# Computing the state-space branch output by block products, with token sums beside the other branches

## The chip, the cores and the metric

The kernel runs on one core of one Trainium2 chip. Its time is that of one execution on the device, in microseconds, as the median over repeated runs. Besides the timed runs there is one execution taken by the hardware profiler. All rows of the profile below come from that single execution, and it has a time of its own, given beside the span of its instructions in the table further down.

## The reference, cut to what matters

One layer of a streaming encoder runs over 1024 tokens of width 1024 in float32. A projection feeds three branches (latent attention, forgetting attention and a state-space scan) and a gate for each. The branch outputs are merged with sigmoid gates, projected and added to the input. A gated feed-forward block follows.

```python
y_a = mla_branch(u_mla, ...) @ w_br_mla[l]          # 512 inner columns
y_b = fox_branch(u_fox, ...) @ w_br_fox[l]          # 512 inner columns
y_c = ssm_branch(u_ssm, ...) @ w_br_ssm[l]          # 1024 inner columns
merged = g[:, :, 0] * y_a + g[:, :, 1] * y_b + g[:, :, 2] * y_c
x = x + merged @ w_out[l]
x = x + conv_ffn(rms_norm(x, norm_ffn_g[l]), ...)
```

`ssm_branch` ends in `rms_norm(y * silu(z), norm_g)`, so its last step is a multiplication of each of the 1024 inner columns by its own element of `norm_g`. The change concerns this scale and the three products with `w_br_fox`, `w_br_mla` and `w_br_ssm`, above all the last.

## The kernel before, in words

Every matrix product keeps float32 accuracy by splitting both operands into a rounded high half and the remainder, its low half. A product over one block of 128 inner rows is then three matmuls, high by high, high by low and low by high (`mm3`, L161 to L168, whose matmuls all have L167). A split is `split` (L139): ScalarE copies the source into the high half (L142) and VectorE subtracts that from the source to give the low half (L143). Inner dimensions are cut in blocks of 128 partitions, tokens in halves of 512 columns.

The stages follow each other on TensorE: input projections, attention, the scan, the branch products, the output projection (`wo`, L1443) and the feed-forward. The gate projections are a generator, `all_fill` (L866), whose matmuls are laid between those of attention and scan. Its last ones run behind the scan's last. Each gate block ends in a tanh on ScalarE (L873) that takes its bias from the constant tile `pc_g`, and in a store to `g_d`.

The scan handles 8 chunks of 128 tokens. `ssd_c` (L1237 to L1245) ends each: eight 128x128 transposes into two PSUM tiles (L1242), one ScalarE copy of each PSUM tile into the tile `yT` (L1243), and a store of `yT` to the DRAM tile `ys_d` (L1245). `yT` has one buffer; `ssd_b` of the next chunk uses it for a square (L1229), which therefore waits for the store.

The branch stage (L1269 to L1312) follows. For branch 1 (fox), 0 (mla) and 2 (state-space) it first loads the branch's output in blocks of 128 rows by 1024 tokens (`ar`, L1283) and splits each into `ah` and `al`; for branch 2 the split multiplies by the column of `pc_n` (L1287, L1288). Then it goes through 8 output tiles of 128 columns. Each takes a load and split of a weight tile (`load_w`, L758, into `wr`, `wh`, `wl`, two buffers each), a load of the gate (`gl`, L1298), and per token half a product into one of six PSUM banks (`ybr`), with 12 matmuls for branches 1 and 0 and 24 for branch 2. VectorE multiplies by the gate (L1305). GpSimd adds for branch 0 (L1308) and VectorE for branch 2 (L1310). For branch 2 the sum is split into `hnh` and `hnl` (L1311, L1312), which the output projection reads. In all these are 2x8x2x12 + 8x2x24 = 768 matmuls of 128x512.

The tiles `ar`, `gl` and the gate projections' results share one tag, `t4`, with four buffers of 4 KB per partition. A load into `t4` can be issued only when one of the four is free.

Two kinds of order exist. In a section under `manual_schedule` the named engines run in the order in which the program was written. Everything else, here all of SP's transfers, all of GpSimd, and in the branch stage also TensorE, VectorE and ScalarE, is put in order by the planner before the launch, from its own estimate of when each operation is ready. Each engine then runs its list strictly in that order. The scan holds TensorE alone to the program order. The output projection does the same. In the feed-forward, a product by seven block products per pair of output tiles is in use already (`product`, L1392; sums of weight tiles by GpSimd at L1492 to L1496; `ua`, `ub`, `uc`, `ud` at L1397).

Pools are stacked: when one closes, the next to open lies at the same address. At L1269 `mix` closes, which held `const2` (L62). The pool opened after it begins where `const2` began. In `const2`, allocated in order from L94, `lead2`, `identb`, `ones`, `tri`, `strict`, `mssd`, `mfox` and `mmla` take 3360 bytes per partition, and `pc_g` the next 336. Before the change that place is taken by the first two `merged` tiles, which are written by the first L1305.

## Time and profile before

| | |
|---|---|
| median of 3 runs | 2069.3 us (2063.23 to 2069.39) |
| the profiled execution | 2072.75 us, span of its instructions 2071.0 us |
| TensorE busy | 2016.5 us, 97% of the span, 10250 matmuls |
| VectorE, ScalarE, GpSimd busy | 1432.4 us, 949.4 us, 616.3 us |
| first and last matmul of the branch stage start | 1152.4 us and 1326.6 us |
| mean granted TensorE clock | 0.992 of full speed |

Times in rows are microseconds unless marked ns. `PE` is TensorE, `PEld` its weight load, `DVE` VectorE, `ACT` ScalarE, `POOL` GpSimd, `SP` the engine that issues all transfers and `SPq` its queue. A row of the chain of waits gives a start, a length and what ran. A row of the timeline gives start, length, engine, line, operation, output and inputs, and in brackets the idle time before it and what ended that. A row of the groups by shape gives the count, the total and the mean in ns, and after the next bar the idle time before. A row of the stages gives the stretch, its length, the busy time of PE, PEld, DVE, ACT and POOL with counts, the granted clock, the share of DMA time and GB/s. Matmuls overlap: each is shown with 389 ns, though the next starts earlier. PE busy near the length of a stretch so means that no matmul waited, and the time per matmul is read from a row that holds many.

### The profile page before, as it was taken

The numbers are of one execution on the slowest core, as the hardware profiler recorded it, in microseconds if no ns is written. First come the engines' busy times: TensorE is split into PE (matmuls) and PEld (weight loads), VectorE is DVE, ScalarE is ACT, GpSimd is POOL, SyncE is SP. The second block draws the span as 40 slices with busy tenths as digits, with TensorE's granted clock in tenths as the row PEclk, the third lists the DMA queues.
The fourth block names the chain that finished last, engine by engine and source line by source line (L and its number), as shares of the span: only waits on it lengthen the run. The fifth ranks groups of instructions, "written<-read, shape, count | busy, mean of one in ns | idle before, by whom it ended". The sixth has DMA issues, their size and how long they took to land.

```text
span 2071.0 us, 28992 instructions
## 1 busy us (share of the span) xinstructions
PE 2016.5 (97%) x10250; PEld 1686.1 (81%) x10265; DVE 1432.4 (69%) x2586; ACT 949.4 (46%) x1730; POOL 616.3 (30%) x606
## 2 busy tenths in 40 slices
PE   7999899999999999999999999999899999999999
PEld 7899778788888888787778888888788888878887
DVE  7678479366667767657896355557987777775665
ACT  5555323156556666555554222323454444444432
POOL 4345233222222222210000040002654454422765
PEclk9999999999999999999999999999999999999999
DMA  5158777654434445324442665432222322329675
GB/s 167 45 172 261 260 221 233 204 146 141 118 114 115 130 131 133 100 82 135 134 134 82 215 209 166 153 124 64 77 93 80 96 78 72 102 93 345 218 232 190
DMA packets 274794, 303.62 MB, mean 147 GB/s; under 512 B 18860, under 2 KB 206520, under 8 KB 274648
## 3 DMA queue, kind: packets, MB, share of 16 engines
q1 hardware_dynamic: 274648, 301.76, 47.0%
q8 instruction: 81, 1.33, 0.3%
q14 instruction: 65, 0.53, 0.1%
HBM read 209.03 MB, written 92.67 MB: 146 GB/s over the span
## 4 chain that ended last, share of the span: by engine, by line
PE 81%; DVE 9%; DMA 4%; ACT 2%; issue 2%; POOL 1%; SPq 1%; DVEq 0%; ACTq 0%; POOLq 0%
PE mm L866 17%; PE dn L1729 10%; PE ybr L167 8%; PE ua L1397 5%; PE uc L1397 5%; PE ud L1397 5%; PE fx L167 5%; PE wo L1443 4%; PE s L956 4%; PE tp L1025 3%; PE ub L1397 2%; PE fxv L167 2%; PE q L167 1%; PE kv L167 1%; DMA att_d<-o 1%
## 5 line engine op out<-in xcount | busy, mean ns | idle before, releaser
L866 PE MATMUL mm<-hnh,wh 128*128 128x512 f32 x576 | 250.7, 435 | 0.0
L866 PE MATMUL mm<-hnh,wl 128*128 128x512 f32 x576 | 226.8, 394 | 0.0
L866 PE MATMUL mm<-hnl,wh 128*128 128x512 f32 x576 | 225.4, 391 | 0.0
L978 POOL TENSOR_SCALAR pm<-pm,rs 128x128 f32<-128x128 f32 (+7 forms) x128 | 107.9, 845 | 350.8 <-DVE rs L977 323.7
L1729 PE MATMUL dn<-dr,dr 128*128 128x512 f32 x592 | 182.1, 389 | 0.0
L1031 DVE TENSOR_TENSOR ptl<-tp,pth 128x512 fp32r<-128x512 f32 (+1 forms) x160 | 101.4, 634 | 84.7 <-ACT pth L1030 83.8
L961 DVE TENSOR_REDUCE nmx<-s 128x1 f32<-128x128 f32 (+2 forms) x192 | 105.8, 551 | 58.3 <-PE s L959 46.7
L971 ACT ACTIVATE pm<-s,nmx 128x128 f32<-128x128 f32 (+2 forms) x192 | 109.6, 575 | 56.9 <-DVE nmx L968 38.1
L1729 PEld LDWEIGHTS dn<-dr,dr 128*128 128x128 f32 x592 | 111.2, 188 | 23.0
L866 PEld LDWEIGHTS mm<-hnh,wl 128*128 128x128 f32 x576 | 108.2, 188 | 24.9
L866 PEld LDWEIGHTS mm<-hnl,wh 128*128 128x128 f32 x576 | 109.2, 190 | 18.4 <-issue 4.1
L866 PEld LDWEIGHTS mm<-hnh,wh 128*128 128x128 f32 x576 | 108.9, 189 | 17.8 <-issue 4.1
L1030 ACT ACTIVATE pth<-tp 128x512 fp32r<-128x512 f32 (+1 forms) x160 | 88.2, 551 | 70.4 <-PE tp L1025 69.6
L956 PE MATMUL s<-qk,qk 96*128 96x384 f32 (+5 forms) x480 | 118.1, 350 | 1.9 <-DMA qk<-q_l 0.9
L1308 POOL TENSOR_TENSOR mg<-mg,gl 128x512 f32<-128x512 f32 x16 | 24.9, 1558 | 306.8 <-DVE gl L1305 306.7
L1729 PE MATMUL dn<-dr 128*128 128x512 f32 x296 | 115.3, 389 | 0.0
L143 DVE TENSOR_TENSOR dr<-dr,dr 128x1024 fp32r<-128x1024 f32 x52 | 75.1, 1446 | 50.5 <-ACT dr L142 39.1
L167 PE MATMUL fx<-w5h,hnh 128*128 128x512 f32 x256 | 102.2, 399 | 2.5 <-ACT w5h L142 2.5
L167 PE MATMUL fx<-w5l,hnh 128*128 128x512 f32 x256 | 100.6, 393 | 2.0 <-DVE w5l L143 2.0
L167 PE MATMUL fx<-w5h,hnl 128*128 128x512 f32 x256 | 100.5, 393 | 0.0
L167 PE MATMUL ybr<-al,wh 128*128 128x512 f32 x256 | 99.2, 390 | 0.1
L167 PE MATMUL ybr<-ah,wl 128*128 128x512 f32 x256 | 98.3, 389 | 0.0
(502 smaller groups left out, 5820.9 us busy)
## 6 DMA issues: line engine op xcount, KB each, us to landing
dr<-act_d SPq DMA_DIRECT2D x99, 256.0 KB
wr<-in_ffn_w_up_dram SPq DMA_DIRECT2D x47, 512.0 KB
wr<-in_w_in_dram SPq DMA_DIRECT2D x36, 512.0 KB
g_d<-t SPq DMA_DIRECT2D x24, 512.0 KB
gl<-g_d SPq DMA_DIRECT2D x24, 512.0 KB
ws<-in_ffn_w_down_dram SPq DMA_DIRECT2D x22, 512.0 KB
wsum_d<-ws SPq DMA_DIRECT2D x22, 512.0 KB
act_d<-fa SPq DMA_DIRECT2D x22, 512.0 KB
```

The lines of the kernel that those rows point to most:

```text
L143: return i, le.tensor_sub(l, src, f32(h))
L167: T.matmul(ps, a(k), b(k), start=(i == 0), stop=(i == n - 1))
L866: T.matmul(ps, a[:, k, :], b[half][:, k, :], start=(k == 0 and i == 0), stop=(k == NK - 1 and i == 2))
L956: T.matmul(ps[:, :w], q_[:, qs], k_[:, a:a + w], start=i_ == 0, stop=not last and i_ == len(o.passes) - 1)
L961: later(c + 0.1, lambda ps=ps, ci=ci, a=a, b=b: V.reduce_max(nmx[:, ci:ci + 1], ps[:, :b - a], axis=AX, negate=True))
L971: pss[ci][1][0] = later(c + 0.9 + 0.1 * ci, lambda ci=ci, a=a, b=b: A.activation(p_[:, a:b], pss[ci][0][:, :b - a], AF.Exp, bias=nb, accum ...
L978: G.tensor_scalar(p_[:, 0:n * P], p_[:, 0:n * P], rs[:, 3:4], 0.0, op0=ALU.mult, op1=ALU.add)
L1030: later(c + 0.05, lambda th=th, pt=pt, off=off: A.activation(th[:, :off], pt[:, :off], AF.Copy))
L1031: pl[0] = later(c + 0.6, lambda th=th, tl=tl, pt=pt, off=off: V.tensor_sub(tl[:, :off], pt[:, :off], f32(th[:, :off])))
L1397: T.matmul(ps, a, b, start=first and n == 0, stop=n == 11, skip_group_check=not first)
L1443: T.matmul(p, a, b, start=k == 0 and i == 0, stop=k == NK - 1 and i == 2)
L1729: T.matmul(ps[m], a[:, ts_], b[:, 512:], start=first_ and j == 0 and q == 0, stop=j == NFH - 1 and q == 2, skip_group_check=not first_)
```

## The change

The product of the state-space branch is regrouped. Output tiles j and j+4 (for j from 0 to 3) form a pair. The two weight tiles, each cut into two halves of the inner dimension, and the tokens, cut into two halves of inner rows and of 512 tokens, form a 2x2 by 2x2 block product, done by seven `product` calls of 12 matmuls in place of eight blocks: `a0` (two), `b0` (one), `c0_` (two) and `d0` (two). Sums of weight blocks (`weight_sums`, four GpSimd operations of 128x512 per pair) and sums of token blocks (`tsum[1]` to `tsum[4]`) are the operands; the temporaries `e1`, `f`, `e5`, `X` and `Y` put the results together. The last pair's accumulated tiles are rounded into `mh` and `ml` for the output projection by `rounded`; the tiles of the pairs before it are rounded there too.

The token sums are formed while branches 1 and 0 run. In each of the 16 steps s, `sums_load(s)` loads 4 blocks of 128x128 from `ys_d` by two transfers and subtracts on GpSimd; in step s+1 `sums_take` makes two splits of 128x256 and two subtractions of 128x128 on VectorE. They go into the `hn` tiles that the gate projections read before. Branch 0's blocks are loaded in steps 2 to 5 (`whole`), half of the plain state-space blocks in steps 9 to 12 (`tok_block`), the first pair's weights in step 15.

TensorE, VectorE and ScalarE now keep program order in the whole stage (from the fourth pair's second product on TensorE alone). Branch 1's four blocks are loaded ahead of that section. The operands lie in new pools `slot0` to `slot3` of four 4 KB tiles each, opened before the `mg` pools: `slot0` and `slot1` hold branch 1's high and low halves, then the blocks of token half 0; `slot2` and `slot3` branch 0's.

The scale by `pc_n` moves into the scan's end: the copy of each PSUM tile into `yT` becomes four copies of 128x128, each with its column as scale.

```diff
                 pt = psp.tile([P, 512], F32, name=uid("stp"), tag="ts", bufs=2)
                 for j in range(4):
                     T.transpose(pt[:, j * P:j * P + P], yf[:, (4 * g + j) * P:(4 * g + j + 1) * P], ident)
-                A.activation(o.yT[:, 4 * g:4 * g + 4, :], pt.rearrange("p (j s) -> p j s", j=4), AF.Copy)
+                for j in range(4 * g, 4 * g + 4):
+                    A.activation(o.yT[:, j, :], pt[:, j % 4 * P:j % 4 * P + P], AF.Copy, scale=pc_n[:, j:j + 1])
                 yield 0.44
             SY.dma_start(ys_d[:, :, c * P:c * P + P].rearrange("j p s -> p j s"), o.yT)

...
     mix.close()
+    def product(ps, hl, k0, rh, rl, first=True):
+        n = 0
+        for k in range(4):
+            h, l = hl[0][:, k0 + k, :], hl[1][:, k0 + k, :]
+            for a, b in ((h, rh[k]), (h, rl[k]), (l, rh[k])):
+                T.matmul(ps, a, b, start=first and n == 0, stop=n == 11, skip_group_check=not first)
+                n += 1
+
...
+
+    def weight_sums(S12, S34, ri, rj):
+        G.tensor_add(S12[:, 0:4, :], rj[:, 0:4, :], rj[:, 4:8, :])
+        G.tensor_sub(S12[:, 4:8, :], S12[:, 0:4, :], ri[:, 0:4, :])
+        G.tensor_sub(S34[:, 0:4, :], ri[:, 0:4, :], rj[:, 0:4, :])
+        G.tensor_sub(S34[:, 4:8, :], ri[:, 4:8, :], S12[:, 4:8, :])
+
     with ExitStack() as pe_:
+        slots = [pe_.enter_context(TP(f"slot{i}", 1)) for i in range(4)]
         mgs = [pe_.enter_context(TP(f"mg{i}", 1)) for i in range(4)]
-        mp_ = pe_.enter_context(TP("mgp", 1))
+        trp = pe_.enter_context(TP("tr", 1))
         psp = pe_.enter_context(TP("pse", 6, space=PSUM))
         merged = [mgs[j // 2].tile([P, S], F32, name=f"mg{j}", tag=f"mg{j}") for j in range(NK)]
+
+        def slot(i, shape, d=F32R):
+            return slots[i].tile(shape, d, name=uid("op"), tag="op", bufs=4)
...
         mh, ml = alloc_hn()
-        for b, wsrc, nk in ((1, w_br_fox, 4), (0, w_br_mla, 4), (2, w_br_ssm, 8)):
-            ah, al = [], []
-            for k in range(nk):
-                raw = fpl.tile([P, S], F32, name=uid("ar"), tag="t4", bufs=4)
-                SY.dma_start(raw, ys_d[k] if b == 2 else att_d[b][k * P:k * P + P, :])
-                h = mp_.tile([P, S], F32R, name=uid("ah"), tag="ah", bufs=8)
-                l = mp_.tile([P, S], F32R, name=uid("al"), tag="al", bufs=8)
-                if b == 2:
-                    A.activation(h, raw, AF.Copy, scale=pc_n[:, k:k + 1])
-                    V.scalar_tensor_tensor(out=l, in0=raw, scalar=pc_n[:, k:k + 1], in1=f32(h),
-                                           op0=ALU.mult, op1=ALU.subtract)
-                else:
-                    split(h, l, raw)
-                ah.append(h)
-                al.append(l)
-            wv = wsrc[0].rearrange("(k p) c -> p k c", p=P)
...
-                    V.scalar_tensor_tensor(out=m if b == 1 else g[:, hs], in0=g[:, hs], scalar=1.0, in1=ps,
-                                           op0=ALU.add, op1=ALU.mult)
-                    if b == 0:
-                        G.tensor_add(m, m, g[:, hs])
...
+
+        def sums_load(n):
+            k, q = n // 4, n % 4 * P
+            r = pieces[n] = trp.tile([P, 4, P], F32, name=uid("tr"), tag="tr", bufs=3)
+            for i in range(2):
+                SY.dma_start(r[:, 2 * i:2 * i + 2, :],
+                             ys_d[k + 4 * i].rearrange("p (h c) -> p h c", h=2)[:, :, q:q + P])
+            G.tensor_sub(r[:, 0:2, :], r[:, 1:4:2, :], r[:, 0:2, :])
+
+        def sums_dst(n, a):
+            k, q = n // 4, n % 4 * P
+            return mh[1 - a][:, k:k + 5:4, q:q + P], ml[1 - a][:, k:k + 5:4, q:q + P]
+
+        def sums_take(n, a):
+            r = pieces[n]
+            if a:
+                V.tensor_sub(r[:, 3, :], r[:, 3, :], r[:, 0, :])
+                V.tensor_sub(r[:, 2, :], r[:, 2, :], r[:, 3, :])
+            split(*sums_dst(n, a), r[:, 2 * a:2 * a + 2, :])
+
+        def tok_block(k, half, sl, raw=None):
+            if raw is None:
+                raw = fpl.tile([P, 2, 512], F32, name=uid("ar"), tag="t4", bufs=4)
+            SY.dma_start(raw, ys_d[k:k + 2, :, 512 * half:512 * half + 512].rearrange("k p c -> p k c"))
+            h, l = slot(sl, [P, 2, 512]), slot(sl, [P, 2, 512])
+            split(h, l, raw)
+            return [(h[:, i, :], l[:, i, :]) for i in range(2)]
+
+        def whole(b, k):
+            raw = fpl.tile([P, S], F32, name=uid("ar"), tag="t4", bufs=4)
+            SY.dma_start(raw, att_d[b][k * P:k * P + P, :])
+            h, l = slot(2 * (1 - b), [P, S]), slot(2 * (1 - b) + 1, [P, S])
+            split(h, l, raw)
+            return h, l
+
...
+        def rounded(js, half):
+            for j in js:
+                m = merged[j][:, 512 * half:512 * half + 512]
+                A.activation(mh[half][:, j, :], m, AF.Copy, scale=0.5)
+                V.scalar_tensor_tensor(out=ml[half][:, j, :], in0=m, scalar=0.5, in1=f32(mh[half][:, j, :]),
+                                       op0=ALU.mult, op1=ALU.subtract)
+
+        def operand(raw):
+            h, l = (fpl.tile([P, NK, P], F32R, name=uid(n), tag=n) for n in ("wh", "wl"))
+            split(h, l, raw)
+            return h, l
+
+        def add(o, src, c, half):
+            hs = slice(512 * half, 512 * half + 512)
+            V.scalar_tensor_tensor(out=o.g[c][:, hs], in0=o.g[c][:, hs], scalar=1.0, in1=src,
+                                   op0=ALU.add, op1=ALU.mult)
+            V.tensor_add(merged[c][:, hs], merged[c][:, hs], o.g[c][:, hs])
+
+        def pair_raws(j):
+            o = Head()
+            o.j, o.r = j, [fpl.tile([P, NK, P], F32, name=uid("wr"), tag="wr") for _ in range(2)]
+            for r, c in zip(o.r, (j, j + 4)):
+                SY.dma_start(r, wvs_ssm[:, :, c * P:c * P + P])
+            return o
+
+        def pair_sums(o):
+            o.S12, o.S34 = (fpl.tile([P, NK, P], F32, name=uid(n), tag="t4", bufs=4) for n in ("S12", "S34"))
+            weight_sums(o.S12, o.S34, *o.r)
+
+        def first_operands(o):
+            if o.j:
+                o.hA = operand(o.r[0])
+            o.h22 = last22[:, 0:4, :], last22[:, 4:8, :]
+            split(*o.h22, o.r[1][:, 4:8, :])
+
+        heads = {1: [whole(1, k) for k in range(4)], 0: []}
+        ready = {0: weights(0)}
+        blocks = []
+        order1 = tc.manual_schedule(engines=MANUAL)
+        order1.__enter__()
+        for s in range(2 * NK):
+            b, j = 1 - s // NK, s % NK
+            if s + 1 < 2 * NK:
+                ready[s + 1] = weights(s + 1)
+            g = fpl.tile([P, S], F32, name=uid("gl"), tag="t4", bufs=4)
+            SY.dma_start(g, g_d[b][j])
+            sums_load(s)
+            if s:
+                sums_take(s - 1, 0)
+            wh, wl = ready.pop(s)
+            for half in range(2):
+                hs = slice(512 * half, 512 * half + 512)
+                ps = psp.tile([P, 512], F32, name=uid("ybr"), tag="half")
+                mm3(ps, lambda k: wh[:, k, :], lambda k: wl[:, k, :],
+                    lambda k: heads[b][k][0][:, hs], lambda k: heads[b][k][1][:, hs], 4)
+                m = merged[j][:, hs]
+                V.scalar_tensor_tensor(out=m if b == 1 else g[:, hs], in0=g[:, hs], scalar=1.0, in1=ps,
+                                       op0=ALU.add, op1=ALU.mult)
+                if b == 0:
+                    G.tensor_add(m, m, g[:, hs])
+                if half == 0 and s:
+                    sums_take(s - 1, 1)
+                if half == 0 and 2 <= s < 6:
+                    heads[0].append(whole(0, s - 2))
+                if half == 0 and 9 <= s < 13:
+                    blocks += tok_block(2 * (s - 9), 0, (s - 9) // 2)
+                if half == 0 and s == 2 * NK - 1:
+                    o = pair_raws(0)
+                    o.hA = operand(o.r[0])
+                    pair_sums(o)
...
+        temps = [slot(3, [P, 2, 512], F32) for _ in range(3)]
+        (e1, f), (e5, X), (Y, _) = ([t[:, i, :] for i in range(2)] for t in temps)
+        last22 = slot(3, [P, NK, P])
+        first_operands(o)
+        for a in range(2):
+            sums_take(2 * NK - 1, a)
+        Y11, Y21 = ([[blk[i] for blk in blocks[4 * n:4 * n + 4]] for i in range(2)] for n in range(2))
+        for j in range(4):
+            tail = j == 3
+            a0, d0, c0_, b0 = (halfbank() for _ in range(4))
+            product(a0, o.hA, 0, *Y11)
+            A.activation(e1, a0, AF.Copy)
+            if tail:
+                order1.__exit__(None, None, None)
+                order1 = tc.manual_schedule(engines={mybir.EngineType.PE})
+                order1.__enter__()
+            o.g = {}
+            for c in (j, j + 4):
+                o.g[c] = fpl.tile([P, S], F32, name=uid("gl"), tag="t4", bufs=4)
+                SY.dma_start(o.g[c], g_d[2][c])
+            o.hS12 = operand(o.S12)
+            product(d0, o.h22, 0, *tsum[4])
+            A.activation(f, d0, AF.Copy)
+            if j == 0:
+                last = [tok_block(k, 1, 2, t) for k, t in zip((4, 6), temps[1:])]
+                Y22 = [[blk[i] for blk in last[0] + last[1]] for i in range(2)]
+            product(a0, o.hA, 4, *Y21, first=False)
+            o.hS34 = operand(o.S34)
+            add(o, a0, j, 0)
+            if tail:
+                rounded(range(4), 0)
+            else:
+                nxt = pair_raws(j + 1)
+                pair_sums(nxt)
+            product(c0_, o.hS12, 0, *tsum[1])
+            A.activation(e5, c0_, AF.Copy)
+            G.tensor_sub(Y, e5, f)
+            product(b0, o.hS12, 4, *tsum[2])
+            V.tensor_add(X, b0, e1)
+            if tail:
+                rounded((4, 5, 6), 0)
+            else:
+                first_operands(nxt)
+            product(c0_, o.hS34, 4, *Y22, first=False)
+            V.tensor_add(e1, c0_, X)
+            add(o, e1, j, 1)
+            if tail:
+                rounded(range(4), 1)
+            product(d0, o.hS34, 0, *tsum[3], first=False)
+            V.tensor_add(e5, d0, X)
+            G.tensor_add(Y, Y, e5)
+            add(o, e5, j + 4, 0)
+            if tail:
+                rounded((7,), 0)
+            add(o, Y, j + 4, 1)
+            if not tail:
+                o = nxt
+        rounded(range(4, NK), 1)
+        order1.__exit__(None, None, None)
```

43 lines of the change are left out of this document (13 added, 30 removed).

## The prediction

> **What bounds the kernel now.** I read the page first, then the chain of waits around the stage that changes, then the stages' busy times.
>
> ```profile
> span 2071.0 us, 28992 instructions
> PE 2016.5 (97%) x10250; PEld 1686.1 (81%) x10265; DVE 1432.4 (69%) x2586; ACT 949.4 (46%) x1730; POOL 616.3 (30%) x606
> ```
>
> TensorE is busy nearly all the time, so what counts is how many matmuls there are and where it stops. The chain of waits from the scan's end to the output projection:
>
> ```profile
> 1145.00 0.36 SPq L1245
> ...
> 1145.41 5.25 DMA ar<-att_d
> ...
> 1150.69 1.07 ACT ah L142
> ...
> 1151.78 1.24 DVE al L143
> ...
> 1153.06 173.96 PE ybr L167 x766
> 1327.02 27.20 PE wo L1443 x120
> ```
>
> 766 matmuls in 173.96 us are 0.2271 us each, without a break. So the stage is bound by TensorE alone, and a matmul taken out is worth 0.2271 us as long as nothing else becomes late. The stretches of branches 1, 0 and 2 say the same of the other engines:
>
> ```profile
> 1152.20:1200.50 48.30, 48.23 (x213) 39.60 (x212) 25.18 (x33) 13.13 (x17) 0.00 (x0) 1.00 0.70 223
> 1200.50:1243.00 42.50, 42.50 (x190) 35.18 (x189) 22.06 (x27) 10.42 (x12) 23.05 (x16) 1.00 0.63 201
> 1243.00:1326.80 83.80, 83.80 (x371) 69.44 (x370) 47.15 (x61) 24.69 (x33) 1.80 (x1) 1.00 0.45 145
> ```
>
> VectorE has about half of its time free, ScalarE more, and transfers take 0.45 to 0.70.
>
> **Part 1, the products.** Branch 2 had 8 x 2 x 24 = 384 matmuls; four pairs of seven products of 12 are 336. 48 fewer, at 0.2271 us: **-10.9 us**. This is the whole gain there can be.
>
> **Part 2, the start.** TensorE's order becomes that of the program: step 0 needs in its first 12 matmuls all four blocks of branch 1, high and low. Before, the planner laid the blocks' first matmuls of four products side by side, since three multiplications by the gate come at once, at 1162.50. How the blocks arrive, in the timelines of SP, ScalarE, VectorE and TensorE:
>
> ```profile
> 1142.20 0.37 SPq L760 DMA_DIRECT2D wr<-in_w_br_fox_dram  x1
> 1145.41 2.75 SPq L1283 DMA_DIRECT2D ar<-att_d  x3
> 1153.03 0.32 SPq L1283 DMA_DIRECT2D ar<-att_d  x1
> 1152.57 1.06 ACT L142 ACTIVATE ah<-ar 128x1024 fp32r<-128x1024 f32 x1 [0.82 <-DMA ar<-att_d]
> 1154.06 0.67 ACT L873 ACTIVATE t<-mm,pc_g 128x512 f32<-128x512 f32 x1
> 1156.46 1.06 ACT L142 ACTIVATE ah<-ar 128x1024 fp32r<-128x1024 f32 x1 [0.79 <-DMA ar<-att_d]
> 1157.56 1.23 DVE L143 TENSOR_TENSOR al<-ar,ah 128x1024 fp32r<-128x1024 f32 x1 [0.63 <-ACT ah L142]
> 1162.50 1.88 DVE L1305 SCALAR_TENSOR_TENSOR mg<-gl,ybr 128x512 f32<-128x512 f32 x3 [3.72 <-PE ybr L167]
> 1152.15 0.39 PE L866 MATMUL mm<-hnh,wl 128*128 128x512 f32 x1
> ```
>
> Three blocks are sent for at once. The fourth has no free `t4` buffer until the first block's low half is done (1151.78 + 1.24 = 1153.02; issue at 1153.03), and is there at 1156.46, 3.43 us later. So even with the times of before the last low half ends at 1157.56 + 1.23 = 1158.79, two matmuls follow it, and the first 12 are issued by 1159.24. Unhindered they would run from 1152.37 (one matmul after the last `mm`) to 1155.10: a stop of 4.1 us that before did not have.
>
> It gets worse by the new place of the operands. `slot0`'s first tile covers bytes 0 to 4095 of the closed `const2`, and `pc_g` (3360 to 3695) is the bias of the last gate tanh. So block 0's high half can't be written until that tanh is over. It needs the last `mm` (1152.15 + 0.39), takes 0.67: 1153.2. Then 1.07 for the high half, 1.24 for the low: 1155.5. Only then is a buffer free; + 3.43 for the transfer, + 1.07 + 1.24 for the fourth block: 1161.3, and the twelfth matmul is issued by 1161.7. The stop is **+6.6 us**, my value. Bounds: 2.9, if the first three loads are issued ahead of the store of `ys_d` (the rival below); 9.5, if the transfer takes the 5.25 us of the first block and block 1 goes ahead of block 0 on ScalarE (1.1 more).
>
> A stop can cost the clock as well. The only long wait of TensorE behind a running product, in the feed-forward's start (waits of TensorE, then stages):
>
> ```profile
> PE uc L1397 <- ACT e L1611: 3.8, 1, 3.8
> PE ud L1397 <- DVE wl L143: 1.5, 1, 1.5
> 1486.00:1490.00 4.00, 1.82 (x4) 1.50 (x5) 3.96 (x4) 2.61 (x4) 2.66 (x2) 0.60 0.10 31
> 1490.00:1494.00 4.00, 4.00 (x11) 3.09 (x10) 3.26 (x3) 0.72 (x1) 2.84 (x2) 0.55 0.04 17
> 1494.00:1498.00 4.00, 4.00 (x19) 3.33 (x18) 4.00 (x3) 2.22 (x3) 3.92 (x4) 1.00 0.35 132
> ```
>
> After 3.8 us of waiting the granted clock is 0.55 until about 1494, and 11 matmuls run where 4.00 / 0.2271 = 17.6 fit. From 1488.2 to 1494 that loses some 5.8 x 0.45 = 2.6 us. The new start is not one gap but several: block 0's high half at 1154.3, its low half at 1155.5, the following blocks about 1.2 apart, and 3.4 before the last. I take 0 for the clock; with 2.6 it is a rival of its own. The Trainium skill, page "TensorE: Matmul & The Clock Gate", section "What's actually happening", has the clock fall after an idle window of about 3.4 us; by that rule the last gap alone would do it and the sum would be 2.6 us higher, while by the rows a wait of 1.5 us does nothing and one of 3.8 us does, which leaves 3.4 open.
>
> **Part 3, the steps of branches 1 and 0.** Durations by shape, on VectorE, ScalarE and GpSimd:
>
> ```profile
> L143 DVE TENSOR_TENSOR wl<-wr,wh 128x512 fp32r<-128x512 f32 x16 | 11.7, 734 | 7.4 <-ACT wh L142 7.4
> L1305 DVE SCALAR_TENSOR_TENSOR gl<-gl,ybr 128x512 f32<-128x512 f32 x32 | 21.8, 686 | 47.5 <-PE ybr L167 39.8 <-issue 4.7 <-POOL mg L1308 3.0
> L1202 DVE TENSOR_TENSOR y<-y,py 128x256 f32<-128x256 f32 x30 | 12.5, 416 | 4.7 <-PE py L1200 4.7
> L1171 DVE TENSOR_TENSOR cbm<-pcb,tri 128x128 f32<-128x128 f32 x13 | 3.7, 287 | 0.0
> L1308 POOL TENSOR_TENSOR mg<-mg,gl 128x512 f32<-128x512 f32 x16 | 24.9, 1558 | 306.8 <-DVE gl L1305 306.7
> L1172 ACT ACTIVATE bT<-pcb 128x128 f32<-128x128 f32 x13 | 3.6, 276 | 11.9 <-DVE cbm L1171 11.9
> L1243 ACT ACTIVATE yT<-stp 128x512 f32<-128x512 f32 x16 | 9.5, 595 | 7.8 <-PE stp L1242 7.6
> ```
>
> A step is 24 x 0.2271 = 5.45 us of TensorE. VectorE has in it one weight half (0.73), two gate multiplications (1.37), two halves of 128x256 for the sums (0.83), two subtractions of 128x128 (0.57), and in eight steps a block of 128x1024 (1.24): 3.5 or 4.7 us. ScalarE needs less. In program order the next weights' halves stand behind the previous step's last gate multiplication and ahead of this step's sums; they end about 1.6 us into the step and are wanted at its end, 5.45, so a late sum or block (SP's transfer, then GpSimd's subtraction) is free up to 3.8 us. Cost **0**, hidden under TensorE. GpSimd has a subtraction more (under 1.56) beside two additions.
>
> Transfers per step: weights 262 kB, gate 524, sums 262, in eight steps a block of 524: 1.05 or 1.57 MB. The first stretch above moved 223 GB/s at a share of 0.70, 319 at full share; 1.57 MB take 4.9 of 5.45 us. It fits with little room; if it ran over, the lead of about one step that four `t4` buffers give has to cover it. Value 0, bound 2 us (eight steps over by a quarter).
>
> **Part 4, the pairs.** TensorE: 7 x 2.72 = 19.1 us a pair. VectorE: three operands of 128x1024 (3.7), `h22` (0.7), eight operations for the merge (5.5), `X`, `e1`, `e5` (2.1): 12.0. That the scheme can keep TensorE fed, the feed-forward shows, with more VectorE work per product:
>
> ```profile
> 1518.66 2.72 PE uc L1397 x12
> ```
>
> The nearest in time is `hS34`: its buffer is `hA`'s, free after the third product, and it is wanted two products (5.4 us) later; 1.07 + 1.24 are needed. **0**, bound 2. In the last pair VectorE has 16 roundings (11 us) on top, but the output projection's first 36 matmuls (8.2 us) want only four of them. **0**, bound 1.5.
>
> **Part 5, the scan.** Four copies of 128x128 for one of 128x512: 4 x 0.276 - 0.595 = 0.51 us more, twice a chunk. ScalarE has the room; but `yT`'s store is 0.5 to 1.0 us later, and the next chunk's square waits for it:
>
> ```profile
> ACT yT L1229 <- DMA ys_d<-yT: 8.1, 6, 3.3
> PE stp L1242 <- ACT y L1234: 0.5, 1, 0.5
> ```
>
> TensorE waited for the end of that chain once, 0.5 us. From nothing to 8 x 1.0; I take **+0.5**, by the second row, as gate matmuls cover the rest.
>
> Sum: -10.9 + 6.6 + 0.5 = **-3.8 us**. The profiled execution would go from 2071.0 to 2067.2 us of span. It took 2072.75 us in all, 3.45 more than the median of the runs shown, 2069.3; against that median I forecast **2065.5**. Its own range: -6.8 (start 4.1, scan 0) to +0.1 (start 9.5, scan 1.5), so 2062.5 to 2069.4.
>
> **Rivals.** *The start is covered.* Between 1142.57 and 1145.00 SP issues nothing and waits for `yT`. If the planner, seeing `yT` later, puts the loads ahead of that store, block 0 is there near 1142.6 + 3.43 = 1146.0 and block 1 some 1.9 behind (as 1152.57 is behind 1150.66, where the first transfer ended). Block 1, which needs no tanh, is split by 1150.2, the fourth block comes 3.43 later and is split by 1156.0. Block 0, still behind the tanh, ends at 1155.5; eleven matmuls follow, the last at 1158.0: a stop of 2.9. Sum -10.9 + 2.9 + 0.5 = -7.5: 2061.8. For: no block depends on that store. Against: the planner put them behind it.
>
> *The clock falls at the start.* -3.8 + 2.6 = -1.2: 2068.1.
>
> *GpSimd holds up VectorE: slower.* In steps 8 to 15 GpSimd works 2 x 1.56 and about 0.9 for the sums, 4.0 of 5.45 us. Where it works, VectorE's operations on two SBUF tiles can take twice as long: the same split of sums in the feed-forward takes 1.58 in place of 1.24:
>
> ```profile
> L143 DVE TENSOR_TENSOR wl<-S,wh 128x1024 fp32r<-128x1024 f32 x32 | 50.7, 1583 | 19.9 <-ACT wh L142 19.9
> ```
>
> If all 4.0 us are lost, the steps with a block take 8.7 and the others 7.5: 4 x 3.3 + 4 x 2.0 = 21, less the 3.8 us of lead, 17 us: -3.8 + 17, 2082.5. It decides from 0.75 us lost per step with a block, or 2.0 without. At the feed-forward's ratio, 1.28, the 3.4 us of such operations lose 0.9, a little over the one and far under the other, and the lead swallows it. The Trainium skill, page "SBUF — State Buffer", in its account of the shared port pair, has the loser blocked for the whole instruction; by that rule the full 4.0 could be lost, and by the measured mean 0.9.
>
> **Chances.** Forecast 0.37, covered start 0.30, clock 0.15, GpSimd or another wait as dear 0.18. About 0.3% (6.2 us) is what a measurement of this kernel can tell from no change. Faster by more: 0.27 of the covered start and a fifth of the forecast, 0.34. Slower by more: 0.18. The rest, 0.48, is within. The range goes from the whole of part 1 with a little run noise, 2057, to 2076, part of the way to the last rival.
>
> **What would show it.** Right: 720 branch matmuls at 0.227 us; no matmul for most of 1152.5 to 1161, and TensorE waiting there for the low half of a branch 1 block; the first high half behind the gate tanh; 2.72 us per product after. Wrong: a start with a gap of under 3 us; a granted clock under 1 after it; TensorE waiting for `wl` in steps 8 to 15, or for `hS34`, `h22` or a token block; new waits for `y` in the scan.

## The result, and the profile after

The changed kernel takes 2084.2 us (median of 4 runs, 2081.77 to 2085.45), the one before beside it 2069.35 (4 runs, 2063.23 to 2074.33): the ratio is 1.0078, with a 95% interval of 1.0063 to 1.0093. It is slower by about 15 us, and the forecast was 2065.5. Its profiled execution took 2081.77 us. The head of its page:

```profile
span 2080.1 us, 29232 instructions
PE 2013.3 (97%) x10202; PEld 1678.5 (81%) x10217; DVE 1483.3 (71%) x2668; ACT 976.2 (47%) x1828; POOL 665.8 (32%) x646
```

The 48 matmuls are gone, and the span is 9 us longer. The place shows when the stretches are cut at the same events in both traces: the scan's first transposition, the last matmul of the gate projections, the first matmul of the output projection. Before, scan, branch stage and the rest (stretch, length, busy time of PE, PEld, DVE, ACT, POOL, then granted clock):

```profile
934.60:1152.15 217.55, 215.91 (x1102) 169.48 (x1115) 167.91 (x330) 110.78 (x179) 0.00 (x0) 1.00 0.42 126
1152.15:1326.86 174.71, 174.64 (x770) 144.30 (x769) 94.43 (x120) 48.25 (x62) 24.85 (x16) 1.00 0.56 181
1326.86:2071.02 744.16, 731.93 (x3233) 603.42 (x3231) 530.29 (x525) 320.90 (x379) 318.80 (x190) 0.99 0.41 135
```

The same stretches after, the branch stage also cut at its 48th, 192nd, 384th and 468th matmul:

```profile
927.53:1151.34 223.81, 219.07 (x1102) 171.97 (x1115) 168.09 (x329) 118.04 (x226) 0.00 (x0) 0.98 0.40 121
1151.34:1335.01 183.67, 172.90 (x722) 138.16 (x721) 144.34 (x195) 66.40 (x111) 76.16 (x55) 0.96 0.62 193
1335.01:2080.05 745.04, 732.22 (x3233) 603.33 (x3231) 531.36 (x533) 322.25 (x382) 316.44 (x191) 0.99 0.41 134
...
1151.34:1171.80 20.46, 15.57 (x50) 10.55 (x49) 10.41 (x13) 6.57 (x9) 4.33 (x3) 0.83 0.81 270
1171.80:1204.40 32.60, 32.60 (x145) 27.02 (x144) 25.06 (x46) 11.43 (x22) 4.44 (x6) 1.00 0.79 248
1204.40:1250.10 45.70, 44.39 (x193) 35.81 (x192) 39.48 (x57) 12.94 (x26) 24.32 (x20) 1.00 0.68 203
1250.10:1277.10 27.00, 22.61 (x85) 17.34 (x84) 20.50 (x19) 9.78 (x14) 19.18 (x13) 0.87 0.35 117
1277.10:1335.00 57.90, 57.72 (x254) 47.43 (x254) 48.88 (x62) 25.68 (x40) 23.89 (x15) 1.00 0.52 164
```

The scan grew by 6.3 us, the branch stage by 9.0: 15.2 together (6.26 and 8.96), beside the 14.9 by which the medians differ. The spans differ by less only because the scan begins 7 us earlier in this execution, behind code that the change does not touch. Over all the profiled executions below that moment lies between 925 and 936 us, so from here on stages are compared, and of whole times only those measured side by side.

At 0.2271 us a matmul the five pieces of the branch stage should take 10.9, 32.7, 43.6, 19.1 and, with the step to the output projection, 57.5 us. So the start lost 9.5 us, steps 8 to 15 2.1, the first pair 8.0, the other pairs 0.4. What TensorE waited for (us in total, times, longest):

```profile
PE ybr L167 <- ACT op L142: 3.3, 2, 2.2
PE stp L1242 <- ACT y L1234: 3.1, 1, 3.1
PE ybr L1276 <- ACT wh L142: 2.7, 1, 2.7
...
PE ybr L1276 <- DVE wl L143: 1.7, 2, 1.5
PE ybr L167 <- DVE op L143: 1.5, 2, 0.8
PE ybr L167 <- DVE wl L143: 1.3, 2, 0.8
```

None of these was there before except the one for `y`, at 0.5. Three places, then.

**The start.** The chain of waits is the prediction's nearly word for word: high half of block 0, its low half, only then the fourth block's transfer, its two halves, and the stage runs. The last gate matmul starts at 1151.34.

```profile
1143.53 7.98 PE mm L866 x35
1152.78 1.06 ACT op L142
1153.86 1.24 DVE op L143
1155.12 4.15 DMA ar<-att_d
1159.29 1.06 ACT op L142
1160.38 1.24 DVE op L143
1161.66 45.88 PE ybr L167 x194
```

The eleventh matmul, the first that reads the fourth block's low half, starts at 1161.66, 10.3 us behind the last gate matmul and 7.8 late. The other 1.7 of the 9.5 us are a slow clock: matmuls 0.43 apart until 1165.4.

**The first pair.** The timelines of TensorE, VectorE and GpSimd:

```profile
1250.12 0.39 PE L167 MATMUL ybr<-op,wl 128*128 128x512 f32 x1
1253.16 0.73 PE L1276 MATMUL ybr<-op,wh 128*128 128x512 f32 x2 [2.65 <-ACT wh L142]
1255.40 0.80 PE L1276 MATMUL ybr<-op,wl 128*128 128x512 f32 x1 [1.50 <-DVE wl L143]
...
1250.48 1.23 DVE L1323 TENSOR_TENSOR tr<-tr 128x128 f32<-128x128 f32 x1
1252.19 0.93 DVE L143 TENSOR_TENSOR hnl<-tr,hnh 128x256 fp32r<-128x256 f32 x1 [0.48 <-ACT hnh L142]
1253.14 2.21 DVE L143 TENSOR_TENSOR wl<-wr,wh 128x1024 fp32r<-128x1024 f32 x1
...
1250.26 1.31 POOL L1283 TENSOR_TENSOR S<-wr 128x512 f32<-128x512 f32 x1
```

The last branch product has been issued at 1250.1 and TensorE wants `hA`. VectorE still works on the sums of piece 14 (what `sums_load(14)` loaded), which stand ahead of `hA`, the first pair's weight halves, in program order, and its operations take up to four times as long as in the prediction (1.23 for 0.29, 2.21 for 1.24) because GpSimd is busy. Two waits of 2.7 and 1.5 us, then again matmuls 0.43 apart until 1261: 8 us with a later stop that costs 0.6.

**The scan.** One wait for `y`, 3.1 us, and behind it a granted clock of one half (clock: the third number from the right):

```profile
1069.80:1073.21 3.41, 0.68 (x3) 0.20 (x2) 3.41 (x9) 2.00 (x3) 0.00 (x0) 1.00 0.66 197
1073.21:1076.62 3.41, 3.01 (x14) 3.01 (x15) 0.67 (x3) 1.49 (x5) 0.00 (x0) 0.50 0.00 0
```

### The profile page after: what moved, and what is told of

The parts are those of the page before. It is cut to its first block, busy times and chain, and to the rows that moved or that the text cites. A ratio compares the mean times of both kernels' runs of the same rounds, so it can differ in the third digit from the quotient of the medians.

```text
span 2080.1 us, 29232 instructions
## 1 busy us (share of the span) xinstructions
PE 2013.3 (97%) x10202; PEld 1678.5 (81%) x10217; DVE 1483.3 (71%) x2668; ACT 976.2 (47%) x1828; POOL 665.8 (32%) x646
## 3 DMA queue, kind: packets, MB, share of 16 engines
q8 instruction: 80, 1.31, 0.3%
## 4 chain that ended last, share of the span: by engine, by line
PE 78%; DVE 11%; DMA 4%; ACT 3%; issue 3%; POOL 1%; SPq 1%; DVEq 0%; ACTq 0%; POOLq 0%
PE mm L866 18%; PE dn L1880 10%; PE ua L1276 5%; PE uc L1276 5%; PE ud L1276 5%; PE fx L167 5%; PE s L956 4%; PE wo L1600 4%; PE tp L1025 3%; PE ub L1276 2%; PE fxv L167 2%; PE ybr L167 2%; PE ybr L1276 2%; PE q L167 1%; DMA att_d<-o 1%
## 5 line engine op out<-in xcount | busy, mean ns | idle before, releaser
L1313 POOL TENSOR_TENSOR tr<-tr 128x256 f32<-128x256 f32 x16 | 14.4, 904 | 309.2 <-DMA tr<-ys_d 290.4
L1283 POOL TENSOR_TENSOR S<-wr 128x512 f32<-128x512 f32 x25 | 35.7, 1427 | 194.4 <-DVE wl L143 157.3
L143 DVE TENSOR_TENSOR wl<-S,wh 128x1024 fp32r<-128x1024 f32 x50 | 77.0, 1541 | 26.3 <-ACT wh L142 26.3
```

Source lines behind the costliest of these rows:

```text
L143: return i, le.tensor_sub(l, src, f32(h))
```

## The experiments

Ratios are to the kernel before, with the 95% interval. The losses are in us against 0.2271 per matmul, by the start times of the 48th, 384th, 468th and 720th branch matmul and of the 36th of the output projection; the scan is its whole length.

| kernel | ratio | scan | start | steps | first pair | rest | output proj. |
|---|---|---|---|---|---|---|---|
| changed | 1.0078 (1.0063 to 1.0093) | 223.8 | 9.5 | 2.0 | 8.0 | 0.4 | 0.0 |
| e1 | 1.0100 (1.0084 to 1.0116) | 223.2 | 11.1 | 2.0 | 7.3 | 0.4 | 0.0 |
| e2 | 1.0066 (1.0042 to 1.0090) | 223.4 | 4.9 | 0.2 | 10.0 | 0.4 | 0.0 |
| e15 | 1.0059 (1.0038 to 1.0080) | 224.0 | 6.0 | 1.3 | 8.5 | 0.5 | 0.0 |
| e10 | 1.0065 (1.0047 to 1.0083) | 221.9 | 1.6 | 2.1 | 8.3 | -0.1 | 6.5 |
| e3 | 1.0040 (1.0024 to 1.0056) | 219.6 | 9.5 | -0.1 | 3.1 | 0.5 | 0.0 |
| e8 | 1.0081 (1.0050 to 1.0112) | 223.6 | 10.3 | 2.8 | 8.5 | 0.2 | 0.0 |
| e4 | 1.0079 (1.0062 to 1.0097) | 224.1 | 9.4 | 1.9 | 7.5 | 0.6 | 0.0 |
| e7 | 1.0042 (1.0027 to 1.0058) | 224.0 | 9.6 | -0.2 | 1.9 | 0.6 | 0.0 |
| e6 | 1.0054 (1.0033 to 1.0075) | 217.0 | 10.6 | 0.8 | 10.2 | 0.4 | 0.0 |
| e11 | 0.9987 (0.9976 to 0.9999) | 217.1 | 1.6 | -0.2 | 0.0 | -0.1 | 7.4 |
| e13 | 0.9963 (0.9950 to 0.9976) | 217.1 | 1.5 | -0.2 | 0.0 | 0.8 | 0.0 |

### The start: where the blocks lie (e1)

```diff
+        trp = pe_.enter_context(TP("tr", 1))
         slots = [pe_.enter_context(TP(f"slot{i}", 1)) for i in range(4)]
         mgs = [pe_.enter_context(TP(f"mg{i}", 1)) for i in range(4)]
-        trp = pe_.enter_context(TP("tr", 1))
```

> Theory (the last gate tanh holds back the first high half, because that half is written over pc_g): with the small buffers of the token sums laid ahead of the operands' slots, pc_g is no longer under block 0. The first high half ends before 1152.5 in place of 1153.8, the fourth block is sent for about 2 us earlier, and TensorE's twelfth matmul of the stage comes near 1159.7 in place of 1161.7. Gain about 2 us, 2082.2. Rival (the first high half waits for its transfer or for ScalarE's order): the chain through the first block stays within 0.3 us of the changed kernel's, 2084.2.

The rival holds. The chain of waits of this kernel, whose last gate matmul starts at 1152.61:

```profile
1153.34 0.67 ACT t L873
1154.01 0.95 ACT op L142
...
1156.13 1.23 DVE op L143
1157.83 4.57 DMA ar<-att_d
```

The high half follows the tanh as before, though nothing of `pc_g` lies under it any more: ScalarE's list has the tanh ahead of it. The loads into `tr`, which now lie over `pc_g`, came behind the tanh on SP, and the fourth block with them: 1.6 us worse.

### The start: TensorE's order (e2) and the fourth block's buffer (e15)

```diff
+            if s == 0:
+                early = {(i, half): halfbank() for i in range(2) for half in range(2)}
+                for k in range(4):
+                    for (i, half), ps in early.items():
+                        hs = slice(512 * half, 512 * half + 512)
+                        for n, (wi, xi) in enumerate(((0, 0), (0, 1), (1, 0))):
+                            T.matmul(ps, ready[i][wi][:, k, :], heads[1][k][xi][:, hs],
+                                     start=k == 0 and n == 0, stop=k == 3 and n == 2)
...
```

> Steps 0 and 1 side by side: TensorE takes 12 matmuls of four products with block 0, then 12 with block 1, and so on, so that it does not need the fourth block before the 37th matmul. Theory (the stop at the start comes from TensorE's program order, which wants all four blocks in its first twelve matmuls): matmuls from block 0's low half on, near 1155.2; 36 of them take 8.2 us, so the fourth block at 1161.7 is in time. The stop goes from 7.8 to about 3.6 us, and what is left of the slow clock is under 2 us. Gain 4 to 6 us: 2078 to 2080. Rival (blocks come too late in any order, and the slow clock costs the same): gain under 1.5 us, above 2082.7.

The start lost 4.9 us in place of 9.5. The fourth block is as late as ever, and nobody waits for it: the theory, within its numbers at the start. Two gaps of 2.3 and 1.0 us beyond a matmul's own 0.23, for the first block, stay, and slow matmuls behind them. By the ratios the whole gained only some 2.5 us of the 4 to 6 expected; the first pair lost 2 us more in this execution.

```diff
-            raw = fpl.tile([P, S], F32, name=uid("ar"), tag="t4", bufs=4)
+            if b and k == 3:
+                raw = slot(3, [P, S], F32)
+            else:
+                raw = fpl.tile([P, S], F32, name=uid("ar"), tag="t4", bufs=4)
```

> The changed kernel, with one edit: branch 1's fourth block is read into a tile of slot 3, so that its transfer needs no t4 buffer; the order on ScalarE and TensorE stays. Theory buffer (the prediction's chain: the fourth transfer starts only when the first block's low half is done): the fourth block lies there before the third is split, the four high halves follow the last gate tanh one behind the other, 4 x 1.06, and the twelfth matmul comes some 3 us earlier, about 7.5 us behind the last gate matmul in place of 10.3; the first 48 matmuls lose 6 to 7 us in place of 9.5. Rival (the tanh alone decides, or the transfers are slow right behind the scan's store): 9 us or more stay.

6.0 us, the eleventh matmul (the twelfth, as the expectation counts) 8.3 us behind the last gate matmul in place of 10.3. So the wait for a buffer is a link of the chain, worth 3.6 us with the slow clock that goes with it. What is left begins behind the tanh, where the four high halves now follow each other (ScalarE from 1152.14 to 1156.04).

### The start as a whole (e10)

Four edits: `mgs` opened below the slots, the fourth block's buffer as in e15, `heads[1]` built inside the section of program order (which puts two high halves ahead of the tanh), and step 0's two products taken block by block.

> The changed kernel with its start alone altered: the splits of branch 1's four blocks stand in program order ahead of the second weights', the fourth block is read into a tile of slot 3 so that it waits for no t4 buffer, the sums' output tiles lie below the slots, and step 0 runs its two products side by side, block by block. Theory order (the stop comes from the order on ScalarE, weights and last gate tanh ahead of the blocks, and from the fourth block's buffer): first high half before the last tanh, low halves from about 1.5 us behind the last gate matmul and 1.24 apart, so that the first 48 matmuls of the stage lose 1.5 to 3 us in place of 9.5: 7 us less than the changed kernel, near 1.0045 of the kernel before. Rival (the blocks' transfers are late: 2 MB right behind the scan's last store): the first 48 still lose 6 us or more, gain under 3.

The start lost 1.6 us, as expected. The total gained 2.7 us by the ratios and not 7, as the output projection now waited (row of this kernel's waits):

```profile
PE wo L1618 <- DVE wol L143: 4.7, 1, 4.7
```

With `mgs` at the bottom, the first buffers of the output projection's weights lie over merged tiles that the last roundings still read. e13 tests that.

### GpSimd's additions (e3, e8)

```diff
                 if b == 0:
-                    G.tensor_add(m, m, g[:, hs])
+                    V.tensor_add(m, m, g[:, hs])
```

That is e8. In e3 both lines are left out, and with them the addition.

> The additions of branch 0's products on GpSimd are left out, so that the output lacks branch 0's part; everything else stays. Theory GpSimd (its additions make VectorE's operations on two SBUF tiles two to four times as long): in steps 8 to 15 the 128x128 subtractions fall from 0.8 to 1.3 us to about 0.3, the gate multiplications start within 1.5 us of their product, steps 12 to 14 are 5.45 us each (2.2 us gained), and the wait at the first pair falls from some 7 us to 4 or less: 2078 to 2080. Theory order (VectorE is late because it waits in program order for ScalarE's halves): lag of 3 us and more stays, under 1 us gained: 2083.2 or more.

> The changed kernel with branch 0's sixteen merge additions on VectorE in place of GpSimd: some 0.6 us each by the 128x512 products of VectorE, 1.2 us a step more. Theory GpSimd (its additions cost VectorE more than they would on VectorE itself): VectorE's other operations return to their durations of steps 0 to 7, the first pair and steps 12 to 14 lose 6 us or less in place of 10: 4 us gained or more, under 1.006 of the kernel before. Rival load (VectorE has simply too much to do there): another 1.2 us a step on it make steps 9 to 15 longer, the loss there grows past 13 us, above 1.009.

Without the additions 2.1 us of the steps and 4.9 of the first pair come back. With them on VectorE the loss is 11.3 us, between the 6 and the 13 that were to decide, so neither theory holds alone. VectorE's groups by shape in steps 8 to 15 (count, then total us and mean ns), changed kernel:

```profile
L143 DVE TENSOR_TENSOR hnl<-tr,hnh 128x256 fp32r<-128x256 f32 x15 | 10.1, 670 | 3.4 <-ACT hnh L142 3.4
L143 DVE TENSOR_TENSOR op<-ar,op 128x1024 fp32r<-128x1024 f32 x4 | 6.4, 1601 | 1.0 <-ACT op L142 1.0
L1323 DVE TENSOR_TENSOR tr<-tr 128x128 f32<-128x128 f32 x7 | 5.9, 844 | 0.2
```

With the additions on VectorE (e8):

```profile
L1407 DVE SCALAR_TENSOR_TENSOR gl<-gl,ybr 128x512 f32<-128x512 f32 x15 | 10.2, 680 | 1.1 <-PE ybr L167 1.1
L1410 DVE TENSOR_TENSOR mg<-mg,gl 128x512 f32<-128x512 f32 x14 | 10.1, 722 | 0.5
L143 DVE TENSOR_TENSOR hnl<-tr,hnh 128x256 fp32r<-128x256 f32 x15 | 7.4, 493 | 3.4 <-ACT hnh L142 3.4
L143 DVE TENSOR_TENSOR op<-ar,op 128x1024 fp32r<-128x1024 f32 x4 | 4.9, 1225 | 2.1 <-ACT op L142 2.1
L1323 DVE TENSOR_TENSOR tr<-tr 128x128 f32<-128x128 f32 x7 | 2.0, 292 | 0.2
```

With GpSimd's thirteen additions of this stretch gone from it, the same operations fall from 844 to 292 ns, from 1601 to 1225, from 670 to 493: 3.9 + 1.5 + 2.7, some 8 us over these rows. Two groups that are not shown (the other 128x128 subtraction, L1322, from 534 to 360 ns, and the weights' low halves, from 755 to 685) make it 10. On VectorE the fourteen additions themselves are 10.1 us. One price replaces the other. The stages of the three kernels, from the 192nd to the 384th matmul, say what that means; changed kernel, e3 and e8:

```profile
1204.60:1250.40 45.80, 44.49 (x193) 35.63 (x192) 39.78 (x57) 12.94 (x26) 24.62 (x21) 1.00 0.67 201
```

```profile
1198.10:1241.70 43.60, 43.60 (x193) 35.85 (x191) 32.86 (x58) 13.11 (x26) 9.12 (x10) 1.00 0.72 219
```

```profile
1213.40:1260.00 46.60, 44.34 (x193) 35.62 (x191) 39.09 (x70) 12.94 (x26) 6.02 (x7) 1.00 0.64 193
```

The TensorE time to be covered is 43.6 us. VectorE is busy 39.8 and 39.1 in the two that stall, and by the rows above it also waits for ScalarE's high halves, 3.4 us for `hnh` and 1.0 or 2.1 for `op`: 44.2 and 44.6, more than there is. In e3 it is busy 32.9 and waits 5.1 for halves and blocks: 38.0, and nothing stalls. So the cause is that sum, work plus stretching plus round trips, not GpSimd by itself. The stretching is shown by e3; that the round trips count in full is argued from the sum, as no run takes them away alone. The Trainium skill, page "SBUF — State Buffer", section "SBUF: two separate sides", has a VectorE operation with two inputs in SBUF fully blocked by a GpSimd operation that reads SBUF and started first, for the whole of that operation. The rows agree: the 128x128 subtraction in the first pair starts at 1250.48, 0.22 us behind a GpSimd operation of 1.31 us, takes 1.23 and ends 0.14 behind it, while the gate multiplication, one of whose inputs is in PSUM, keeps its 0.68 us.

### The first pair's operand (e4) and the sums' place (e7)

```diff
+            if s == 2 * NK - 1:
+                o.hA = operand(o.r[0])
             if s:
                 sums_take(s - 1, 0)
...
```

The rows `o.r` are sent for at the end of step 14.

> The first pair's rows are sent for at the end of step 14, and their split (hA) stands at the top of step 15, ahead of the sums of pieces 14 and 15. Theory order (only the operand's place in VectorE's order is at fault): the first pair's first product starts without a stop, about 7 us gained: 2077. Theory load (VectorE as a whole is some 5 us behind there): the stop moves to the second product, which wants piece 15's sums, and 4 to 5 of the 7 us stay: 2081.5 to 2083.

The stop moved to the second product, which wants `h22`; of some 8 us in the first pair 7.5 stay. Load, not order (waits of this kernel in the first pair):

```profile
PE ybr L1276 <- ACT op L142: 2.4, 1, 2.4
PE ybr L1276 <- DVE op L143: 1.4, 1, 1.4
```

In e7 the same edit stands beside another place for the sums: piece n is taken in half-step `AT[n]`, two each in steps 1, 6, 7 and 8, one in steps 0, 2 to 5, 9, 13 and 14, none in 10 to 12 and 15.

```diff
+        AT = (1, 2, 3, 4, 6, 8, 10, 12, 13, 14, 15, 16, 17, 19, 26, 28)
...
+                if 2 * s + half in AT:
+                    n = AT.index(2 * s + half)
+                    sums_take(n)
+                    if n + 3 < 16:
+                        sums_load(n + 3)
...
```

> The changed kernel, with the sixteen token sums moved towards steps 0 to 9 (two left, in steps 13 and 14) and the first pair's rows split at the top of step 15. The merge additions stay on GpSimd. Theory load (in steps 9 to 15 VectorE has more to do than fits, because GpSimd's work stretches it): steps 0 to 15 run without a stop, and the first pair loses under 3 us in place of 8: gain 7 to 9 us, near 1.0035 to 1.0045 of the kernel before. Rival (the pair's own work, h22 and the weight sums on GpSimd, is late whatever is moved): the first pair still loses 5 us or more, gain under 5, above 1.0055.

Steps without a stop, 1.9 us in the first pair: the theory. All of GpSimd's additions are still there. The edit of e4 is part of it; the early sums without it were not run.

### The scan (e5, e6, e12)

e5 is the kernel before with the scan's part of the change alone.

> The kernel before with the scan's part of the change alone: yT is copied in eight pieces scaled by pc_n, and branch 2 splits its blocks unscaled. The prediction's own price for this part is 0.5 us (0 to 8). Theory scan: it is the part that was mis-sized; in the changed kernel's trace the scan, from its first matmul to the last gate matmul, takes 223.8 us against 217.5 before, with one wait of TensorE for y of 3.1 us and a slow clock behind it. So about 6 us more, ratio 1.003. Rival: the longer scan of the changed kernel comes from the stage behind it (other tiles, another order), and this kernel is within 1.5 us of the one before.

Ratio 1.0022 (1.0007 to 1.0036), and the scan takes as long as in the changed kernel, while the branch stage is within 1.1 us of that of before (of the 6 us in the scan the whole shows 4.6):

```profile
926.91:1150.41 223.50, 219.29 (x1102) 171.76 (x1115) 168.18 (x329) 118.49 (x227) 0.00 (x0) 0.98 0.40 122
1150.41:1326.21 175.80, 174.87 (x771) 144.18 (x769) 94.49 (x120) 48.27 (x63) 24.82 (x16) 1.00 0.56 180
```

e6 takes the square's wait for the store away:

```diff
-            A.activation(o.yT.rearrange("p j s -> p (j s)"), yf, AF.Square, accum_out=ss)
+            A.activation(zt, yf, AF.Square, accum_out=ss)
```

> The changed kernel, with the throwaway result of the norm's square written over zt, which is spent by then, and not over yT, whose store may still be reading. Theory store: the square waits for the store of the chunk before, which the eight small copies made later; without that wait TensorE waits 0.5 us or less for y, and the scan takes 217.5 us or less in place of 223.8: about 6 us less than the changed kernel, near 1.005 of the kernel before. Rival order: the chain behind the square is late because of the order on VectorE and ScalarE; the wait for y stays at 2 us or more, and under 2 us are gained.

The scan is 217.0 us, with no wait for `y` and no slow clock, though all 64 small copies are still there. Of the 6.8 us gained in the scan the whole shows 2.4 thousandths, 5 us; the first pair was 2.2 us worse in this execution. The same edit on the kernel before (e12):

> The kernel before, with only the square's throwaway result over zt. Theory: its one wait of TensorE for y, 0.5 us, goes, and nothing else: within 1 us of the kernel before, so that what the combined kernel gains beyond that is the seven products'. Rival: the store's wait also sets the pace of the scan elsewhere, and 3 us or more are gained.

Ratio 0.9998 (0.9983 to 1.0013), scan 216.6: nothing to gain there. The store's wait was free until the copies made it later.

### All cures together (e11, e13)

> All four cures in one kernel: the start just described, the square's throwaway result over zt, the token sums moved towards steps 0 to 9 with the first pair's rows split at the top of step 15, and the two late token blocks of the first pair sent for ahead of its gates. Theory (the losses are separate: 6.3 us in the scan, 9.5 at the start, 2.1 in steps 12 to 14, 8.0 in the first pair, against 10.9 saved by the 48 matmuls): the branch stage takes 166 to 168 us in place of 174.7 before, the scan 217, the whole 7 to 9 us less than the kernel before: ratio 0.9955 to 0.9965. Rival (a cure at one place brings a stop at the next, as when only hA was moved): the stage stays above 170 us, ratio 0.9975 or more.

The branch stage took 165.1 us, better than expected, and the output projection lost 7.4, much as in e10 (6.5), which the expectation had not counted. So only 0.9987 (0.9976 to 0.9999). e13 differs in one line:

```diff
-    ops = [po_.enter_context(TP(f"op{i}", 1)) for i in range(5)]
+    ops = {i: po_.enter_context(TP(f"op{i}", 1)) for i in (4, 0, 1, 2, 3)}
```

> The four cures together once more, and the five buffers of the output projection's weights in another order: the 32 kB that are needed last lie first, over the merged tiles, and the four that are needed first over slots 0 and 1. Theory place (in the kernel with all cures TensorE waited 4.7 us for the output projection's second weights, whose buffers lay over tiles that the last roundings still read; with the slow clock behind it the first 36 matmuls lost 7.4 us): that wait falls under 1 us, the first 36 matmuls lose under 1.5 us, and the kernel is 6 to 7.5 us below the one with all cures, ratio 0.9950 to 0.9965. Rival (those weights come late because SP's queue or VectorE holds them, wherever they lie): 4 us or more stay, ratio 0.9980 or more.

2060.4 us (6 runs) beside 2067.3: ratio 0.9963 (0.9950 to 0.9976), below both kernels. The output projection's loss is gone, which shows the place of its buffers as the cause; by the ratios the whole gained 5 us over e11, not the 6 to 7.5 expected, and the last pairs lost 0.9 us more. Its scan and branch stage:

```profile
935.90:1152.96 217.06, 215.58 (x1101) 169.71 (x1115) 167.97 (x329) 117.85 (x227) 0.00 (x0) 1.00 0.41 125
1152.96:1318.87 165.91, 164.50 (x722) 135.09 (x721) 134.81 (x194) 67.14 (x111) 76.85 (x55) 1.00 0.66 211
```

8.8 us less than before in the branch stage and 0.5 in the scan. The seven products are worth what part 1 said, less 2.1 us of seams.

## Why the prediction was wrong, point by point

**Part 1, the products: right.** 48 matmuls fewer, 0.2271 each: e13 shows 8.8 of the 10.9 us in its branch stage.

**Part 2, the start: right in its mechanism, too small by 2.9 us.** 6.6 was forecast, 9.5 measured: a stop of 7.8 and 1.7 of slow clock, which the prediction had put at 0 and made a rival of. The stop is longer by the fourth transfer (4.15 us in place of 3.43) and by a weight's high half that ScalarE makes ahead of the tanh (0.4). For the clock the prediction looked at stops of 1.5 and 3.8 us alone and left what lies between open; the trace of the kernel before has a fall behind one of 2.42 us (from the matmul at 858.53 to the next). The fourth block's buffer is a link of the chain (e15). One step was not shown: that block 0 waits *because* it lies over `pc_g`. Moving it off changed nothing (e1); ScalarE's list keeps the tanh ahead. Place and order together (e10) brought it forward; order alone was not tried. The rival of the covered start fell: SP kept the blocks behind the store.

**Part 3, the steps: wrong, and the step that failed is "cost 0, hidden under TensorE".** VectorE's work for the sums was added up from rows of the scan, in which GpSimd is idle, and from durations alone. It came to 3.5 or 4.7 of 5.45 us; with the stretching and the waits for ScalarE's halves VectorE had no time left in steps 8 to 15 (44.2 of 43.6 us). There it cost 2.0 us.

**Part 4, the pairs: wrong at the first pair, right behind it.** Cost 0 with a bound of 2, measured 8.0 there and 0.4 in the other three. The prediction looked at `hS34` as the nearest in time, in a pair that finds VectorE on time. The first pair finds it late, with `hA` behind the sums of pieces 14 and 15. That is where the lag of part 3 fell due: `hA` ahead of the sums (e4) leaves 7.5 of the 8.0 us, and the same with the sums taken earlier (e7) leaves 1.9 and no stop in the steps.

**Part 5, the scan: the mechanism seen, the size wrong by more than ten times.** "I take +0.5", measured 6.3, within the bounds that were named (0 to 8). The copies are as estimated: four take 1.14 us in place of 0.60.

```profile
1143.57 1.14 ACT L1244 ACTIVATE yT<-stp,pc_n 128x128 f32<-128x128 f32 x4 [0.67 <-PE stp L1242]
```

But in the chunk that stalls the square starts 4.1 us behind its neighbouring matmul (1060.81 and 1056.72) where it was 1.8 (1064.96 and 1063.20), the wait for `y` grew by 2.6 us, and the slow clock added about 3. The prediction took the delay times the one wait it knew; it did not ask what else in the planner's lists would shift. Two copies explain 1.1 of the 2.3 us; the rest is the store and the lists, and is not taken apart. That it hangs on the store e6 shows.

**The sum.** -10.9 + 9.5 + 2.0 + 8.0 + 0.4 + 6.3 = +15.3, against +14.9 measured. Of the 19 us by which the forecast missed, the scan's term is 5.8, part 4 8.4, part 2 2.9 and part 3 2.0. So the costliest error is VectorE's time in steps 8 to 15, put at 0 and measured at 10.0 us of parts 3 and 4 together (some 2.9 of them slow clock), counted with the first pair where it fell due.

**The rivals.** "GpSimd holds up VectorE" gave 2082.5, 2 us from what came, and its place is right; its price is not, so that its time came near is luck. It had 17 us for the stretching; the additions account for 7 (e3), and the scan and the start, which are not in it, for the rest. "The clock falls at the start" came true as a mechanism and three times over: 1.7 us at the start, some 2.9 in the first pair, some 3 in the scan.

## What to carry to other kernels

Where an order by a planner is replaced by the order of the program, look at the seams first: the first use behind each stage, what stands ahead of it on every engine, and which buffer must come free. An engine's room is not its busy time taken from quiet rows: add what a neighbour's work will stretch and each round trip that it waits for, and carry the lag forward to the next deadline. A wait that is already on the path, even one of 0.5 us, has no margin: price what makes it longer by its full length, and add the slow clock behind it.

## What the runs showed of the hardware

**When the clock falls.** TensorE stood before the same transposition of the scan for a different time in each kernel that has the small copies and the square over `yT`. The gap was 2.33 us from the matmul ahead in e3, where the clock stayed whole. It was 2.87 (e1), 2.95 (e5), 3.04 (e10) and up to 3.77 us (e4) in the nine others, where it fell to one half, for 3.4 us in e10 and for 6.8 in the rest. The scan took 4.9 (e10) to 7.1 us (e4) longer than e6's 217.0.

The length of the stop is not the whole rule. The kernel before lost its clock behind a gap of 2.42 us (at 858.53, busy for 1.26 of the 3.41 us from 858.72 on) and kept it behind one of 2.17 (at 281.57). The granted clock in the traces changes on a grid: apart from the first and the last stretch of an execution, every stretch at one clock is a multiple of 3.41 us, in the changed kernel 6.83 from 1073.21, 3.41 from 1155.13 and from 1161.96, 6.83 from 1254.12. Cut at this grid, the rows of the scan above have TensorE busy for 0.68 of 3.41 us ahead of the fall. In e3 the same two windows are:

```profile
1066.45:1069.86 3.41, 1.69 (x8) 1.08 (x7) 3.41 (x9) 2.24 (x4) 0.00 (x0) 1.00 0.47 157
1069.86:1073.28 3.42, 3.20 (x22) 2.95 (x23) 1.21 (x4) 1.58 (x6) 0.00 (x0) 1.00 0.00 0
```

That is 0.50 of a window, and no fall. In all fifteen profiled executions there are 105 falls: 101 follow a window in which TensorE was busy for less than half, four one of 0.51 to 0.57. Only ten other windows of under one half, all between 0.45 and 0.50, had no fall behind them. So several short stops add up when they lie in one window: 2.55 and 1.26 us in e2 left 0.77 of 3.41 us busy, and the clock fell; 1.87 and 0.92 in e3's first pair left 1.93, and it did not. Where the windows' edges fall is chance. The Trainium skill, page "TensorE: Matmul & The Clock Gate", section "What's actually happening", has the activity counted in free-running windows of about 3.4 us and the clock fall after an idle one. The grid and the two states of full and half agree; here a window that was idle for half of its length was enough.

**Where the additions run hardly matters.** In the stretch from the 192nd to the 384th matmul thirteen of GpSimd's 128x512 additions stretched VectorE's operations by about 10 us; on VectorE fourteen took 10.1. That an engine is free doesn't make work on it free.
